# Split gate weights kept in memory for the second half of the tokens, and the MLP's sums and differences of weights and hidden values made by VectorE instead of GpSimd

## The chip, the cores and the metric

One core of a Trainium2 chip runs the kernel. Its time is in device microseconds (us), the median of three runs. Five engines work beside each other: TensorE (PE, matmuls), VectorE (DVE), ScalarE (ACT), GpSimd (POOL), and SyncE (SP), whose queue issues all loads and stores. Each runs its own list of instructions in order and waits on semaphores for the others.

## The reference

A token sequence x (2048 tokens of width 1024) goes through two blocks. What matters here is the first one, between its state-space mixer and its MLP:

```python
def s5_mixer(u, ..., w_glu):
    ...
    y = jax.nn.gelu(y).astype(u.dtype)
    a, g = jnp.split(y @ w_glu, 2, axis=-1)
    return a * jax.nn.sigmoid(g)

def sqrelu_mlp(h, w1, w2):
    a = jax.nn.relu(h @ w1)
    return (a * a) @ w2

x = x + mix
x = x + sqrelu_mlp(rmsnorm(x, norm_ffn[i]), mlp_w1[i], mlp_w2[i])
```

`w_glu` is 1024 x 2048, `w1` 1024 x 4096, `w2` 4096 x 1024, all float32. A second gate (`ple`) and a whole second block of attention, recurrence and convolution follow, which the change doesn't touch.

## The kernel before

**Numbers.** PE gets float16 operands. Each float32 value v is split into hi = float16(v) and lo = float16(v - hi), weights after a factor of 64 (`WS`). A product needs three matmuls: hi hi, hi lo, lo hi (`product`, line 257). ScalarE makes a hi, VectorE the lo (`stt`, line 58, or `sub`, line 50).

**Tokens and tiles.** Tokens come in four blocks n = 0 to 3 of 512 columns (`TB`); rows of x in eight tiles m of 128 (`KT`).

**The mixer's end** (`ssm`, last lines). The generator `mixer` stops twice near its end. `build` (line 146) puts the first products of the gated unit, `gated(0)`, behind the first stop, then lets the mixer finish (`flip`, line 2203, transposes the last eighth of y and splits it), then `gated(1)`.

**The gated unit** (`glu`, line 362). 32 units (m, n): first half n = 0, 1 for all m, second half n = 2, 3. A unit has 48 matmuls into two of the four banks with tag "b" (`gated`, line 351), then a sigmoid by ScalarE (`sg`, line 373), two operations by VectorE that add the gated product to x, and ScalarE's squares for the next norm, which GpSimd sums (`squares`, line 283). A half uses each of the eight gate weight tiles once; class `Weights` loads a tile as two 512 KB pieces (`ws`), and its jobs split it (`prepare`, line 376: four operations on ScalarE, four on VectorE). Since the list of tiles has the eight gate tiles twice (line 168), the second half loads and splits them again.

**What runs beside it.** Three lists of jobs are worked off a few at a time, at places written by hand: `step` (line 249) takes n pending norm jobs and one weight job; `split_aside` (line 487) takes jobs of `presplit` (line 427), which makes the seven combinations of every w2 tile that the MLP needs: subtractions on GpSimd, hi on ScalarE, lo on VectorE, a store to memory `wd_s`. After the first half `norm_pair` (line 558) queues the norm of blocks 0 and 1: first the reciprocal root (`pair_rstd`, line 519, with empty jobs as delay), then 28 parts of a norm, a difference or both, with a cast and a subtraction each.

**The MLP** (`mlp`, line 670) works on two blocks of tokens at a time with seven products in place of eight (the operands of a 2 x 2 block product are combined beforehand by additions and subtractions). Per half of the tokens there are 16 calls of `up` (line 696; I call one a piece: seven products of 12 matmuls into four banks) and eight of `down` (line 753: four times seven products of six matmuls), in the order up, then up, up, down and so on, with one up ahead of the last down. VectorE evicts every product of `down` from its bank (`sums`, line 772). The seven combined weights of a piece are made by `Weights.combine` (line 418): four additions or subtractions (tile `sw`) by `pool` = GpSimd, seven hi by ScalarE, seven lo by VectorE, as ten jobs, called in the `up` before (`steps`) or in the `down` before. The seven combined hidden values need four subtractions more (`less`, line 703), also by `pool`. In both functions the variable `pool` alone decides the engine. `norms` (line 872) takes the norm jobs of the other half of the tokens in every second step of a `down`, so that three downs per half are crowded with them (`norm_away`, line 601, `norm_parked`, line 876).

**Queues.** All loads and stores are issued by SyncE in program order; a store that waits for VectorE holds up what comes behind it.

## Time and profile before

| | before |
|---|---|
| median of three runs | 3205.69 us (3202.18 to 3206.14) |
| the profiled execution | 3202.28 us, span 3200.5 us |
| mean granted clock of TensorE | 0.989 |
| PE busy | 3096.0 us (97%), 16756 matmuls |
| DVE busy | 2177.6 us (68%), 4485 instructions |
| ACT busy | 1308.2 us (41%), 2827 instructions |
| POOL busy | 620.6 us (19%), 482 instructions |

In the span, the mixer's end and the start of the gated unit lie at 233 to 265 us, the gated unit's first half of the tokens ends near 408, its second half near 605; the MLP runs from 608 to 1810, its second half of the tokens from 1215. A busy time is the sum over an engine's instructions; what PE waits for is read from its timeline, where idle time stands in brackets with the instruction that ended it.

### The profile page before, as it was taken

What the parts mean: (1) busy time and instruction counts of PE and PEld (TensorE: products, weight loads), DVE (VectorE), ACT (ScalarE), POOL (GpSimd) and SP (SyncE); (2) the same over time, 40 slices, a digit from 0 to 9 for tenths busy, and PEclk for the clock granted to TensorE, in tenths of its full rate; (3) what the DMA queues carried; (4) which work ended last, traced back from release to release, by engine and by line L of the source; (5) the groups of instructions that cost most, each with busy time, mean ns of one, the idle gap of its engine ahead of it and who ended that gap; (6) DMA issues with size and microseconds to landing.
All of it is one profiled execution on the core that took longest, in us unless ns stands there. A gap on an engine that the chain in (4) does not pass through costs nothing. (4 is left out here: it accounts for less than half of the span.)

```text
span 3200.5 us, 45638 instructions
## 1 busy us (share of the span) xinstructions
PE 3096.0 (97%) x16756; PEld 1593.0 (50%) x16756; DVE 2177.6 (68%) x4485; ACT 1308.2 (41%) x2827; POOL 620.6 (19%) x482
## 2 busy tenths in 40 slices
PE   8889998899999999999999999999999999999999
PEld 6664443344444444444444444654544446666644
DVE  8995668667776667677655655755767866677742
ACT  8983444444444325333333343311212325555610
POOL 0002443332232325322222334200000000000000
PEclk9999999899999999999999999999999999999999
DMA  4136665524342254344322510241121333233242
GB/s 156 52 112 213 212 219 193 175 73 125 112 128 83 76 186 163 89 119 128 98 84 73 185 33 20 75 140 53 63 70 59 108 105 108 82 85 86 81 151 86
DMA packets 294721, 356.94 MB, mean 112 GB/s; under 512 B 44960, under 2 KB 214880, under 8 KB 291296
## 3 DMA queue, kind: packets, MB, share of 16 engines
q1 hardware_dynamic: 289888, 345.63, 34.2%
q10 hardware_dynamic: 4608, 8.39, 0.7%
q8 instruction: 132, 2.16, 0.3%
q14 instruction: 93, 0.76, 0.1%
HBM read 257.98 MB, written 95.94 MB: 111 GB/s over the span
## 5 line engine op out<-in xcount | busy, mean ns | idle before, releaser
L264 PEld LDWEIGHTS <-w 128*128 128x128 f16 x4032 | 396.4, 99 | 502.4 <-issue 35.2
L711 PE MATMUL up<-y,w 128*128 128x512 f16 x2688 | 586.6, 380 | 6.7 <-ACT w L2460 3.4
L768 PE MATMUL dn<-x,w 128*128 128x512 f16 x1764 | 435.0, 381 | 11.3 <-DVE ss L59 5.0
L768 PEld LDWEIGHTS <-w 128*128 128x128 f16 x2688 | 263.9, 98 | 343.5 <-issue 27.9
L711 PEld LDWEIGHTS <-w 128*128 128x128 f16 x2688 | 263.4, 98 | 326.0 <-issue 6.5
L264 PE MATMUL ga<-y,w 128*128 128x512 f16 x1536 | 342.4, 386 | 23.7 <-ACT sg L373 17.9
L59 DVE SCALAR_TENSOR_TENSOR x<-dn,x 128x512 f32<-128x512 f32 x320 | 217.8, 687 | 75.3 <-PE dn L768 70.5
L768 PE MATMUL dn<-y,w 128*128 128x512 f16 x924 | 252.1, 382 | 8.1 <-DMA w<-wd_s 3.2
L41 DVE TENSOR_TENSOR y<-up,y 128x512 f32<-128x512 f32 x128 | 88.4, 690 | 213.2 <-PE up L711 212.0
L59 DVE SCALAR_TENSOR_TENSOR w<-ws,w 128x512 f16<-128x512 f32 x228 | 186.8, 824 | 21.4 <-ACT w L2406 15.3
L1441 PE MATMUL oz<-oz,h 128*128 128x512 f16 x768 | 190.3, 386 | 0.0
L264 PE MATMUL pg<-h,w 128*128 128x512 f16 x768 | 171.4, 379 | 2.5 <-DVE h L41 2.5
L41 POOL TENSOR_TENSOR r<-y,r 128x512 f32<-128x512 f32 x96 | 139.4, 1452 | 159.3 <-DVE x L41 99.0
L1815 PE MATMUL fo<-mx,wo 128*128 128x512 f16 x768 | 167.4, 379 | 0.0
L264 PE MATMUL wide<-w,h 128*128 128x512 f16 x768 | 166.9, 379 | 0.0
L264 PE MATMUL mqk<-h,w 128*128 128x512 f16 x768 | 165.9, 379 | 0.0
L264 PEld LDWEIGHTS <-h 128*128 128x128 f16 x1152 | 112.4, 98 | 99.5 <-DVE gif L59 4.0
L59 DVE SCALAR_TENSOR_TENSOR acc<-u,par,acc 128x512 f32<-128x512 f32 x232 | 159.2, 745 | 0.0
L41 POOL TENSOR_TENSOR sw<-ws 128x512 f32<-128x512 f32 x64 | 89.4, 1397 | 350.8 <-DMA ws<-w 221.6
L41 POOL TENSOR_TENSOR ss<-ss,sq 128x512 f32<-128x512 f32 x70 | 99.1, 1420 | 269.6 <-ACT sq L292 269.6
L2460 ACT ACTIVATE w<-sw 128x512 f16<-128x512 f32 x128 | 79.1, 623 | 126.6 <-POOL sw L41 126.1
L292 ACT ACTIVATE sq<-x 128x512 f32<-128x512 f32 x84 | 51.9, 628 | 176.5 <-DVE x L41 143.3
(402 smaller groups left out, 4753.1 us busy)
## 6 DMA issues: line engine op xcount, KB each, us to landing
w<-wd_s SPq DMA_DIRECT2D x448, 128.0 KB
ws<-w SPq DMA_DIRECT2D x64, 512.0 KB
wd_s<-pw SPq DMA_DIRECT2D x112, 256.0 KB
ws<-wd SPq DMA_DIRECT2D x34, 512.0 KB
ws<-wglu SPq DMA_DIRECT2D x32, 512.0 KB
pw<-w SPq DMA_DIRECT2D x32, 512.0 KB
y<-hop_s SPq DMA_DIRECT2D x20, 512.0 KB
xu<-xu SPq DMA_DIRECT2D x8, 1024.0 KB
```

Source lines behind the costliest of these rows:

```text
L41: f = lambda: (eng or self.nc.vector).tensor_tensor(out=out, in0=in0, in1=in1, op=op)
L59: f = lambda: self.nc.vector.scalar_tensor_tensor(out=out, in0=in0, scalar=s, in1=in1, op0=op0, op1=op1)
L264: self.nc.tensor.matmul(out=ps, lhsT=wk[p], rhs=xk[q], start=(first and i == 0 and j == 0), stop=(last and i == n - 1 and j == 2))
L292: self.nc.scalar.activation(out=sq, in_=x, func=ACT.Square, **kw)
L711: nc.tensor.matmul(out=ps[name], lhsT=ops[o][:, p, 128 * k:128 * k + 128], rhs=self.operand(o, k, q), start=(first and k == 0 and p + q == 0),
L768: nc.tensor.matmul(out=ps[mp, name], lhsT=w[:, 128 * p:128 * p + 128], rhs=x[:, q], start=(opens and c == 0 and p + q == 0), stop=(c == 1 ...
L1441: nc.tensor.matmul(out=d["bank", g], lhsT=x[:, k, s], rhs=y[:, c], start=(k == 0 and j == 0), stop=(k == 7 and j == 2))
L1815: self.nc.tensor.matmul(out=self.begun[m, n], lhsT=w[:, x, c], rhs=y[:, k], start=(k == 0 and j == 0), stop=(k == KT - 1 and j == 2))
L2460: nc.scalar.activation(out=out[q - 2][:, 0], in_=src[q - 2], func=ACT.Copy, scale=scale)
```

## The change

It does four things. (1) The list holds each gate tile once. After its last use in the first half a split tile is stored to a new memory tensor `wg_s` (`keep`), and the second half loads it from there, split (`again`). (2) The second gate tile is split before the mixer's last transposes; a sigmoid on one column stands ahead of the first gate, and the last of the four transposes uses another bank. (3) `pool` in `mlp` and in `Weights.combine` is VectorE; combine's chain is one job shorter, and the first combine is called two units earlier. (4) The pace of the job lists differs: one norm job less per unit from unit 21 on, one presplit job more in units 16 to 21, fewer empty jobs, both reciprocal roots ahead of both spreads.

```diff
-        tiles = [(self.a["wglu"][i], WS) for i in range(KT)] * 2
+        tiles = [(self.a["wglu"][i], WS) for i in range(KT)]
...
         begun = [self.gated(0)]
+        self.weights.prepare(1)
+        self.weights.run()
         next(mixer, None)
         begun.append(self.gated(1))
+        self.nc.scalar.activation(out=self.small[:, 3, 0:1], in_=self.ones[:, 0:1], func=ACT.Sigmoid)
...
-        w = self.weights.get(KT * (n // 2) + m)
+        w = self.weights.get(m) if n < 2 else self.again[m]
...
-            self.step(2)
-            self.split_aside(2)
+            self.step(2 if at < 21 else 1)
+            self.split_aside(3 if 16 <= at < 22 else 2)
...
+        wg_s = nc.dram_tensor("wg_s", [KT, 128, 2, 2048], F16).ap()
+        self.again = {}
+
+        def again(m):
+
+            t = self.wpool.tile([128, 2, 2048], F16, tag=f"w{(KT + m) % 3}", name="w")
+            nc.sync.dma_start(out=t, in_=wg_s[m])
+            self.again[m] = (t[:, 0], t[:, 1])
+
+        def keep(m):
+            for p, t in enumerate(W.get(m)):
+                nc.sync.dma_start(out=wg_s[m, :, p], in_=t)
+
         for half in range(2):
             for m in range(KT):
                 for n in (2 * half, 2 * half + 1):
                     unit(m, n)
                     if n % 2 == 0:
                         i = KT * half + m + 2
-                        if i < 2 * KT:
+                        if i < KT:
                             W.prepare(i)
-                        elif i == 2 * KT + 1:
+                        elif i < 2 * KT:
+                            again(i - KT)
+                        elif i == 2 * KT:
                             self.combined(0)
+                    elif half == 0:
+                        keep(m)
...
-        return [lambda: None] * 3 + [spread, copy]
+        return [lambda: None] * 2 + [spread, copy]
...
-        pool = nc.gpsimd
+        pool = nc.vector
...
-                up(i, (2, 1, 2, 1, 1, 1, 2) if nxt[0] == "up" else (0,) * 7)
+                up(i, (2, 1, 1, 1, 1, 1, 2) if nxt[0] == "up" else (0,) * 7)
...
-        for f in flip(KT - 1, (0, 4, 8, 12), ("a", 3)):
+        for f in flip(KT - 1, (0, 4, 8), ("a", 3)) + flip(KT - 1, (12,), ("c", 1)):
...
-        pool = nc.gpsimd
+        pool = nc.vector
...
+    def run(self):
+        while self.jobs:
+            self.jobs.pop(0)[1]()
```

**Three places of the lists.** ScalarE at the start of the gated unit, before: the last part of the mixer (`GY`, `yt`), the table for the sigmoid, the first gates (`sg`), and between them the second weight tile (`w<-ws`).

```order
L2198 ACTIVATE GY<-y_2730 128x2x16x16
L2216 CAST y_2822<-yt 128x2x64x4 x4
L373 ACT_TABLE_LOAD
L373 ACTIVATE sg<-ga_2779 128x512
L289 ACTIVATE ss<-x_2328 128x512
L2406 ACTIVATE w<-ws 128x512
L373 ACTIVATE sg<-ga_2852 128x512
```

The same place in the change:

```order
L2222 ACTIVATE GY<-y_2730 128x2x16x16
L2430 ACTIVATE w<-ws 128x512 x4
L2240 CAST y_2835<-yt 128x2x64x4 x4
L191 ACT_TABLE_LOAD
L191 ACTIVATE small<-cst 128x1
L377 ACTIVATE sg<-ga_2779 128x512
L292 ACTIVATE ss<-x_2328 128x512
L377 ACTIVATE sg<-ga_2865 128x512
```

All four parts of the second weight tile and the table stand ahead of the first gate now.

ScalarE in the second half of the gated unit, before, from the gate of unit 24 to the gate of unit 25 (casts of line 542 are the norm's, `pw` are presplit's, `w<-ws` gate weights):

```order
L373 ACTIVATE sg<-ga_4839 128x512
L292 ACTIVATE sq<-x_2904 128x512
L542 CAST pw<-nt 128x512
L542 CAST y_2097<-nt 128x512
L477 ACTIVATE pw<-sw 128x4x128 x2
L542 CAST y_2656<-nt 128x512
L2406 ACTIVATE w<-ws 128x512
L477 ACTIVATE pw<-pw 128x4x128
L542 CAST ss<-nt 128x512
L2406 ACTIVATE w<-ws 128x512
L477 ACTIVATE pw<-sw 128x4x128
L373 ACTIVATE sg<-ga_4936 128x512
```

The same two gates in the change:

```order
L377 ACTIVATE sg<-ga_4827 128x512
L295 ACTIVATE sq<-x_2918 128x512
L566 CAST y_2097<-nt 128x512
L499 ACTIVATE pw<-pw 128x4x128
L499 ACTIVATE pw<-sw 128x4x128
L566 CAST y_2656<-nt 128x512
L499 ACTIVATE pw<-sw 128x4x128
L566 CAST ss<-nt 128x512
L499 ACTIVATE pw<-pw 128x4x128
L377 ACTIVATE sg<-ga_4914 128x512
```

The two weight operations are gone, and three norm casts stand where there were four. VectorE's list between the same two gates shrinks from 15 large operations to 12.

VectorE where a `down` (its evictions are `x<-dn`) is followed by a piece (its evictions are `y<-up`), before:

```order
L59 SCALAR_TENSOR_TENSOR x_2910<-dn,x_2910 128x512
L59 SCALAR_TENSOR_TENSOR w<-ws,w 128x512
L41 TENSOR_TENSOR y_2822<-up,y_2822 128x512 x2
L59 SCALAR_TENSOR_TENSOR w<-ws,w 128x512
L59 SCALAR_TENSOR_TENSOR w<-sw,w 128x512 x2
```

The same place in the change:

```order
L59 SCALAR_TENSOR_TENSOR x_2924<-dn,x_2924 128x512
L59 SCALAR_TENSOR_TENSOR w<-ws,w 128x512
L41 TENSOR_TENSOR sw<-ws 128x512
L59 SCALAR_TENSOR_TENSOR w<-ws,w 128x512
L41 TENSOR_TENSOR sw<-sw,ws 128x512
L41 TENSOR_TENSOR y_2835<-up,y_2835 128x512 x2
L59 SCALAR_TENSOR_TENSOR w<-sw,w 128x512 x2
```

Two operations on freshly loaded weights (`sw<-ws`, `sw<-sw,ws`), which were GpSimd's, now stand on VectorE ahead of the piece's first evictions.

## Rows read from the trace of the kernel before

**Rows 1.** Stretches: PE, PEld, DVE, ACT, POOL busy (count), granted clock, DMA share, GB/s.

```profile
265.00:517.00 252.00, 252.00 (x1177) 116.01 (x1176) 177.32 (x230) 108.53 (x194) 105.28 (x71) 0.99 0.64 209
517.00:605.00 88.00, 69.70 (x292) 29.71 (x290) 64.73 (x85) 35.52 (x63) 28.27 (x19) 0.90 0.59 197
605.00:660.00 55.00, 49.28 (x219) 22.00 (x220) 40.69 (x47) 30.02 (x54) 28.26 (x19) 0.94 0.36 107
660.00:1170.00 510.00, 503.41 (x2336) 228.99 (x2334) 350.69 (x532) 199.89 (x343) 145.26 (x107) 1.00 0.37 110
1170.00:1215.00 45.00, 39.08 (x171) 16.81 (x170) 34.70 (x49) 15.61 (x27) 25.82 (x19) 0.96 0.64 211
...
1765.00:1810.00 45.00, 40.11 (x171) 17.13 (x169) 35.77 (x50) 17.66 (x31) 18.99 (x14) 0.92 0.66 217
```

**Rows 2.** Timeline of PE, start of the gated unit: start, us, instruction, [idle before <-releaser].

```profile
260.15 0.60 PE L264 MATMUL ga<-y,w 128*128 128x512 f16 x2 [3.41 <-ACT w L2406]
263.21 37.09 PE L264 MATMUL ga<-y,w 128*128 128x512 f16 x158 [2.46 <-DVE w L59]
```

**Rows 3.** Timeline of PE, end of the gated unit and start of the MLP.

```profile
519.01 10.52 PE L264 MATMUL ga<-y,w 128*128 128x512 f16 x48 [1.21 <-ACT sg L373]
534.42 12.57 PE L264 MATMUL ga<-y,w 128*128 128x512 f16 x48 [4.90 <-ACT sg L373]
548.81 10.52 PE L264 MATMUL ga<-y,w 128*128 128x512 f16 x48 [1.82 <-ACT sg L373]
564.84 12.72 PE L264 MATMUL ga<-y,w 128*128 128x512 f16 x48 [5.51 <-ACT sg L373]
582.01 22.57 PE L264 MATMUL ga<-y,w 128*128 128x512 f16 x96 [4.45 <-ACT sg L373]
607.95 1.03 PE L711 MATMUL up<-y,w 128*128 128x512 f16 x2 [3.38 <-ACT w L2460]
609.39 32.93 PE L711 MATMUL up<-y,w 128*128 128x512 f16 x142 [0.40 <-DVE w L59]
```

**Rows 4.** Stretch of 10 us behind a wait for a sigmoid, columns as in rows 1.

```profile
530.00:540.00 10.00, 5.58 (x17) 2.09 (x17) 8.20 (x11) 4.24 (x8) 3.41 (x2) 0.66 0.35 123
```

**Rows 5.** Timeline of DVE, second half of the gated unit.

```profile
518.99 0.69 DVE L59 SCALAR_TENSOR_TENSOR sg<-ga,sg 128x512 f32<-128x512 f32 x1 [0.49 <-ACT sg L373]
...
530.44 1.75 DVE L41 TENSOR_TENSOR nt<-nt 128x512 f32<-128x512 f32 x1
...
581.99 0.69 DVE L59 SCALAR_TENSOR_TENSOR sg<-ga,sg 128x512 f32<-128x512 f32 x1 [2.36 <-ACT sg L373]
```

**Rows 6.** Groups by line and form: busy us, mean ns of one, idle before.

```profile
L59 DVE SCALAR_TENSOR_TENSOR x<-dn,x 128x512 f32<-128x512 f32 x320 | 217.8, 687 | 75.3 <-PE dn L768 70.5 <-DMA w<-wd_s 1.2 <-DVE x L59 0.5
...
L59 DVE SCALAR_TENSOR_TENSOR w<-ws,w 128x512 f16<-128x512 f32 x228 | 186.8, 824 | 21.4 <-ACT w L2406 15.3 <-ACT w L2460 5.9
...
L41 POOL TENSOR_TENSOR r<-y,r 128x512 f32<-128x512 f32 x96 | 139.4, 1452 | 159.3 <-DVE x L41 99.0 <-DVE y L41 47.3 <-DVE small L41 5.8
```

**Rows 7.** Stretches of a crowded and a plain down call, columns as in rows 1.

```profile
817.00:857.00 40.00, 36.98 (x171) 16.61 (x170) 37.65 (x55) 11.97 (x21) 11.24 (x8) 1.00 0.55 163
...
1043.00:1079.30 36.30, 36.30 (x169) 16.45 (x168) 27.47 (x40) 8.24 (x14) 10.52 (x8) 1.00 0.38 110
```

**Rows 8.** Timelines of DVE and PE at the end of the MLP's first half.

```profile
1179.29 1.08 DVE L41 TENSOR_TENSOR y<-r,y 128x512 f16<-128x512 f32 x1 [2.03 <-ACT y L701]
...
1181.03 1.44 PE L768 MATMUL dn<-x,w 128*128 128x512 f16 x3 [3.12 <-DVE ss L59]
```

**Rows 9.** Timelines of PE, SP and POOL where a piece follows a down call.

```profile
1006.78 3.40 PE L711 MATMUL up<-y,w 128*128 128x512 f16 x15
...
1008.34 0.35 SPq L2373 DMA_DIRECT2D ws<-w  x1
...
1012.20 1.26 POOL L41 TENSOR_TENSOR sw<-ws 128x512 f32<-128x512 f32 x1 [16.82 <-DMA ws<-w]
```

**Rows 10.** Timeline of SP's queue, second half of the gated unit.

```profile
579.66 10.19 SPq L473 DMA_DIRECT2D wd_s<-pw  x3
```

More of the change, by code (lines that the diff above doesn't have):

```diff
@@ L367, in unit @@
         def unit(m, n):
+            at = next(units)
             if m == 0 and n < len(begun):
@@ L377, in unit @@
             self.squares(m, n, m == 0)
-            self.step(2)
-            self.split_aside(2)
+            self.step(2 if at < 21 else 1)
+            self.split_aside(3 if 16 <= at < 22 else 2)
         W.prepare(1)
         self.presplit()
+        units = iter(range(32))
+        wg_s = nc.dram_tensor("wg_s", [KT, 128, 2, 2048], F16).ap()
[7 more added lines that the diff above has]
+                nc.sync.dma_start(out=wg_s[m, :, p], in_=t)
         for half in range(2):
@@ L515, in copy @@
             self.nc.scalar.copy(out=self.rb[n % 2], in_=r["ps"])
-        return [lambda: None] * 3 + [spread, copy]
+        return [lambda: None] * 2 + [spread, copy]
     def pair_rstd(self, na, ss):
-        jobs = [lambda: None] * 4
+        jobs = [lambda: None] * 2
         self.rb = {}
-        for n in (na, na + 1):
-            y = self.r1[:, 4 * n:4 * n + 4]
-            jobs += self.rstd_jobs(ss[n], self.ones[:, 0:1], D, y) + self.spreads(n, y)
+        y = {n: self.r1[:, 4 * n:4 * n + 4] for n in (na, na + 1)}
+        for n in y:
+            jobs += self.rstd_jobs(ss[n], self.ones[:, 0:1], D, y[n])
+        for n in y:
+            jobs += self.spreads(n, y[n])
         return jobs
@@ L850, in mlp @@
                     self.combined(nxt[1])
-                    n = 10
+                    n = 9
                 down(i, n, last, sums_a if i < 8 else sums_b)
@@ L2452, in part @@
         def part(q):
[L2453 to L2454 removed]
+            if q > 1:
+                t, x = out[q - 2], src.pop(q - 2)
                 k.stt(t[:, 1], x, scale, t[:, 0], ALU.mult, ALU.subtract)
[L2456 removed]
+                if q == 8:
                     free(1)
[L2458 to L2460 removed]
+            if 0 < q < 8:
+                out.append(place(q - 1))
+                nc.scalar.activation(out=out[q - 1][:, 0], in_=src[q - 1], func=ACT.Copy, scale=scale)
             if q < 7:
@@ L2464, in part @@
                     free(0)
-        self.jobs += [(i, lambda q=q: part(q)) for q in range(10)]
+        self.jobs += [(i, lambda q=q: part(q)) for q in range(9)]
+    def run(self):
+        while self.jobs:
+            self.jobs.pop(0)[1]()
     def get(self, i):
```

6 lines of the change are left out of this document (removed).

## The prediction

> **What bounds the kernel now.** The first view is the table of stretches [rows 1]. TensorE (PE) is the engine that sets the time: from 265 to 517, through most of the gated unit, it is busy 252.00 of 252.00 us, in the MLP's first half 503.41 of 510. What can be won is the time in which PE stands still or runs slowly, and that sits in few places: 18.3 us idle in the last units of the gated unit (517 to 605, granted clock 0.90 on average), 5.7 us behind it, some 5 us at each of the two ends of an MLP half (1170 and 1765). PE's timeline names the waits. At the start of the gated unit PE waits 3.41 us for ScalarE's and 2.46 us for VectorE's half of the second weight tile [rows 2]. In those last units it waits five times for a sigmoid, 1.21 + 4.90 + 1.82 + 5.51 + 4.45 = 17.89 us, and then 3.38 and 0.40 us for the first weights of the MLP [rows 3]. The granted clock falls to the lower level (1.2 GHz) after such gaps: 0.66 on average between 530 and 540, where PE had just stood still [rows 4]. What this costs is read from PE's rows: 48 matmuls take 10.52 us, but 12.57 and 12.72 behind two gaps [rows 3].
>
> Why the sigmoid is late: VectorE's timeline has the gate products of five following units, the first at 518.99 and the last at 581.99, so 63.0 us for four units, 15.75 us each [rows 5], against 10.5 us of matmuls. VectorE's list has 15 to 18 large operations per unit there, 16.5 on average, thus 0.955 us per operation with all waits. ScalarE's sigmoid stands behind casts that wait for VectorE's results. Part of the 0.955 is GpSimd: beside a GpSimd operation a VectorE operation with two operands in SBUF takes 1.75 us (at 530.44) instead of 0.69 [rows 5].
>
> **The change, part by part** (against the profiled execution: 3202.3 us; the median of the three runs, 3205.7, lies 3.4 above).
>
> *Start of the gated unit.* The second tile is split before the last transposes, in ScalarE time that was idle, and the sigmoid's table is loaded ahead. Gone are 3.41 + 2.46 us, and the slow stretch behind them: 158 matmuls took 37.09 us where 158/48 x 10.52 = 34.6 would do, 2.5 us [rows 2, 3]. Sum 8.4; the unit now waits for banks instead, a few tenths, so I take 8 (bounds 5 to 9).
>
> *Second half of the gated unit.* The split of eight tiles (32 ScalarE, 32 VectorE operations) disappears, and the norm's jobs are spread: three per unit from the end of unit 20 on, instead of four from unit 21 (units counted from 0 to 31). By the new list units 20 to 27 have 11, 13, 12, 13, 12, 13, 12, 12 large VectorE operations, 98 in all: 98 x 0.955 = 93.6 us, against 8 x 10.5 = 84.0 us of matmuls. VectorE thus falls 9.6 us behind, and PE may be one unit ahead (four banks, two per unit), 10.5 us, before it stops. So the waits nearly vanish. What they cost now is 17.89 us, plus the slow stretches 2.05 + 2.20 + 1.5 (22.57 for 96 matmuls, 21.0 when fast) = 23.7 us [rows 3]. At 1.05 us per operation 102.9 - 84.0 - 10.5 = 8.4 us of waits would be left, at 0.9 none: I take 22, which leaves 1.7 (bounds 12 to 23.7).
>
> *Loads and stores.* Instead of 16 loads of 512 KB the second half gets eight of 1 MB: the same bytes. The first half also writes 8.4 MB: 168 us long some 50 GB/s more, on 209 GB/s at a DMA share of 0.64 [rows 1], so about 0.79: hidden. On SyncE's queue the new load of tile m waits for the matmuls of tile m-3, long done when it is its turn, and it has more than two units (21 us) before its first use; the stores wait for nothing new. Cost 0, as long as the queue isn't late by that much.
>
> *First MLP piece.* Its weights are now made from two units earlier on, so 3.38 + 0.40 us and the slow stretch behind (32.93 us for 142 matmuls, 31.1 when fast: 1.8) go [rows 3]: 5.6, I take 5.5 (bounds 2 to 6).
>
> *MLP.* Each of 32 pieces moves eight operations from GpSimd (1.45 us each [rows 6]) to VectorE (0.69): 256 x 0.69 = 177 us more for VectorE in 1200 us. In a plain down call this is hidden: VectorE has 27.47 us of work in 36.30, with seven more operations 32.3 [rows 7]. In the crowded ones (three per half, where a norm runs beside) it is not: 37.65 us in 40, with PE already stopped for 3 us [rows 7], now +4.8 us. Against that, fewer operations are stretched: weight operations take 0.824 on average, those that read a bank 0.687 [rows 6], so some 28 operations with two SBUF operands give back up to 28 x 0.14 = 3.9. That leaves 1 to 2 us per call; PE pays perhaps half of it: six calls, 4.5 us. In the first three pieces VectorE is busy 40.69 of 55 us [rows 1] and gets some 16 operations (11 us): another 1.5. Loss 6 (bounds: gain 4, loss 25).
> At the end of each half the last piece's sums are made in a chain over three engines: VectorE waits 2.03 us for a cast that waits for GpSimd, and PE 3.12 us for the bank behind it [rows 8]. Three GpSimd steps become shorter by some 0.6 us each: 1.8 per half, less what the four new operations take in the first: gain 2 (bounds -2 to 7).
>
> The Trainium skill (SBUF — State Buffer, "Who interferes with whom") calls the port that VectorE and GpSimd share an exclusive lock: the later one stands still for the other's whole instruction. The 1.75 us agree with it at single operations. By that rule the moved operations could free up to 256 x 1.45 = 371 us of VectorE against the 177 us added, and the MLP would gain; this is the second rival.
>
> Sum: 8 + 22 + 0 + 5.5 - 6 + 2 = 31.5 us. 3202.3 - 31.5 = 3170.8; with the 3.4 us to the median **3174 us**.
>
> **Rivals.**
> 1. *The gated unit stays VectorE-bound.* For it: the 0.955 us include presplit's GpSimd subtractions, which stay. At 1.05 us per operation 8.4 us of waits remain and with them two slow stretches (4 us), 12.4 instead of 1.7: 3174 + 11 = 3185.
> 2. *The MLP's own waits go too.* For it: the stretched operations above. Idle there now: 6.6 + 5.9 + 4.9 = 17.4 us [rows 1]. If VectorE gets lighter in effect, these and my loss of 6 go: 3174 - 23 = 3151. Against it: VectorE's evictions read a bank and aren't stretched (0.687 on average [rows 6]).
> 3. *A new wait on VectorE: slower.* GpSimd waited for the weight loads at no cost: after the down call the next piece starts at 1006.78, its second half tile is requested at 1008.34, and GpSimd's addition starts at 1012.20 [rows 9]. Now VectorE makes this addition, and stands still from about 1008.3 to 1012.2, 3.9 us, in 16 pieces, with the evictions of the piece queued behind. The first of these is ready three products (7.8 us) after the start, and PE needs that bank for its sixth product, 13 us after the start; with 3.5 us of work ahead of that, the wait reaches PE if the load lands later than 9.5 us after the start. Measured are 5.4. If it does, each of 16 pieces pays up to 3.9 us: 62 us, 3174 + 62 = 3236. The Trainium skill (Perfetto Trace Analysis, "Optimizing Scalar/DVE Operations") advises to move work to other engines, GpSimd even, where VectorE is saturated, which is the opposite direction; in the crowded calls the trace has VectorE at 37.65 of 40 us [rows 7].
> 4. *The kept tiles come back too late.* In before's second half the queue stands behind stores that wait for VectorE, three of them for 10.19 us [rows 10]. If six of eight loads were late by 4 us, some 24 us would be gone: 3198.
>
> **How the numbers follow.** Forecast 0.55, rivals 0.17, 0.15, 0.07, 0.06. The range reaches from 3159 to 3194: it holds the forecast with its bounds and the first rival, and leaves out most of the second, the third and the fourth. A difference of 0.2% (6.4 us) can be told from none. Faster by more: 0.55 + 0.17 + 0.15 and half of the fourth, 0.90; within: 0.03; slower: 0.07.
>
> **What would show it.** Right: no wait of PE for a weight tile around 260; at most one or two waits for a sigmoid and no fall of the clock between 500 and 600; the first piece without a wait for weights; VectorE's operations in the MLP at 0.69 us, waits of VectorE for weight loads of some 3 us at pieces behind a down call, with PE unaffected; in the crowded down calls PE waits a little longer than before. Wrong: VectorE waits that PE repeats in each piece (third rival), sigmoids that stay late (first), an MLP without any waits (second).

## The result and the profile after

The changed kernel takes 3163.07 us (median of 4 runs, 3160.66 to 3166.15); the kernel before, run beside it, 3204.6 (4 runs). The ratio is 0.9874 (95% interval 0.9862 to 0.9887): 41.5 us faster. Forecast were 3174, in a range from 3159 to 3194. In the profiled executions the span falls from 3200.5 to 3158.9 us, by 41.6.

| | before | after |
|---|---|---|
| mean granted clock of TensorE | 0.989 | 0.995 |
| PE busy | 3096.0 us (97%) | 3081.4 us (98%) |
| DVE busy | 2177.6 us, 4485 instructions | 2248.0 us, 4709 instructions |
| ACT busy | 1308.2 us, 2827 instructions | 1296.6 us, 2796 instructions |
| POOL busy | 620.6 us, 482 instructions | 265.2 us, 226 instructions |

All comparisons below are made by stages. A stage is measured on PE's timeline, from its first matmul to the first of the next stage; the gated unit's units have 48 matmuls each, a piece 84, a down call 168. "Rest of first half" runs from the MLP's second piece to the last down of that half, "second half" from piece 16 to its last down.

| us | to unit 0 | units 0-2 | 3-19 | 20-31 | first piece | rest of first half | its last down | second half | its last down | behind |
|---|---|---|---|---|---|---|---|---|---|---|
| before | 233.3 | 42.6 | 178.6 | 153.4 | 21.3 | 540.7 | 44.6 | 550.5 | 44.7 | 1390.7 |
| after | 233.5 | 32.8 | 178.6 | 135.9 | 18.1 | 536.3 | 43.2 | 547.3 | 42.8 | 1390.4 |
| difference | +0.1 | -9.8 | 0 | -17.4 | -3.1 | -4.5 | -1.5 | -3.2 | -1.9 | -0.3 |

Of the 17.4 us in units 20 to 31, 3.5 belong to the last unit, in which PE no longer waits for the MLP's first weights. So the gated unit gave 23.7 us, the first piece 6.7, the other MLP stages 11.1.

The stretches of the changed kernel that answer to [rows 1, 7] (PE, PEld, DVE, ACT, POOL busy (count), granted clock, DMA share, GB/s): most of the gated unit; its late units; the MLP's first three pieces; a crowded and a plain down call; the two last downs.

```profile
265.00:487.00 222.00, 222.00 (x1046) 102.83 (x1045) 145.19 (x189) 91.25 (x160) 99.28 (x70) 1.00 0.77 261
487.00:581.00 94.00, 85.78 (x387) 38.17 (x386) 83.32 (x100) 39.35 (x70) 33.34 (x21) 0.98 0.55 190
581.00:636.00 55.00, 55.00 (x261) 25.41 (x259) 41.08 (x74) 33.31 (x58) 1.40 (x2) 1.00 0.41 133
711.20:750.40 39.20, 36.57 (x170) 16.43 (x169) 38.76 (x63) 12.03 (x21) 0.00 (x0) 1.00 0.55 153
1008.30:1044.60 36.30, 36.30 (x170) 16.47 (x169) 30.47 (x48) 8.40 (x14) 0.00 (x0) 1.00 0.39 110
1135.20:1178.40 43.20, 39.06 (x170) 16.85 (x169) 37.96 (x55) 15.27 (x26) 14.72 (x10) 0.96 0.64 214
1725.70:1768.50 42.80, 38.87 (x170) 16.85 (x169) 38.10 (x54) 17.73 (x31) 13.71 (x10) 0.96 0.69 227
```

PE is busy without a gap to 487 and again from 581 to 636. What is left lies between 487 and 581 (8.2 us idle), in crowded down calls (2.6 us in the one shown) and at the two ends.

PE's timeline at the start of the gated unit, to be held against [rows 2]: no wait is left, only the last transposes between two runs of products.

```profile
233.47 9.24 PE L267 MATMUL ga<-y,w 128*128 128x512 f16 x42
242.54 1.91 PE L2236 MATMUL yt<-cst,GY 128*128 128x128 f32 x16
244.29 167.22 PE L267 MATMUL ga<-y,w 128*128 128x512 f16 x774
```

PE's timeline at the gated unit's end and the MLP's start, to be held against [rows 3]: the five waits for a sigmoid are shorter, not gone (1.16 + 2.42 + 1.47 + 2.38 + 0.79 = 8.22 us instead of 17.89), one slow unit is left (12.21 us for 48 matmuls), and the MLP's first piece starts without a wait.

```profile
498.94 10.52 PE L267 MATMUL ga<-y,w 128*128 128x512 f16 x48 [1.16 <-ACT sg L377]
511.88 10.52 PE L267 MATMUL ga<-y,w 128*128 128x512 f16 x48 [2.42 <-ACT sg L377]
523.87 10.52 PE L267 MATMUL ga<-y,w 128*128 128x512 f16 x48 [1.47 <-ACT sg L377]
536.77 12.21 PE L267 MATMUL ga<-y,w 128*128 128x512 f16 x48 [2.38 <-ACT sg L377]
549.77 31.24 PE L267 MATMUL ga<-y,w 128*128 128x512 f16 x144 [0.79 <-ACT sg L377]
580.84 26.06 PE L735 MATMUL up<-y,w 128*128 128x512 f16 x120
```

Two readings of the new profile raise the questions. First, why VectorE is still late in the gated unit. It already comes late into it: the gate product of unit 20 stands at 461.32, 5.9 us behind the end of that unit's matmuls. ScalarE's and GpSimd's timelines there:

```profile
452.25 0.63 ACT L499 ACTIVATE pw<-pw 128x512 f16<-128x512 f32 x1 [4.47 <-DMA wd_s<-pw]
...
460.18 0.63 ACT L499 ACTIVATE pw<-sw 128x512 f16<-128x512 f32 x1 [3.79 <-POOL sw L41]
460.71 0.58 ACT L377 ACTIVATE sg<-ga 128x512 f32<-128x512 f32 x1
```

```profile
458.88 1.27 POOL L41 TENSOR_TENSOR sw<-pw 128x512 f32<-128x512 f32 x1 [9.01 <-DMA pw<-w]
```

`presplit` (three jobs per unit now) waits here for its own stores and loads, and the sigmoid stands behind its casts. That is not new in kind: between 265 and 475 us ScalarE's `pw` operations waited 59.0 us for these stores before, and 61.4 us now.

Second, why the MLP got faster by 11.1 us behind its first piece, where the forecast was 4 us slower.

### The profile page after: what moved, and what is told of

It is laid out like the page before. It is cut to its first block, busy times and chain, and to the rows that moved or that the text cites. A ratio compares the mean times of both kernels' runs of the same rounds, so it can differ in the third digit from the quotient of the medians.

```text
span 3158.9 us, 45408 instructions
## 1 busy us (share of the span) xinstructions
PE 3081.4 (98%) x16756; PEld 1589.5 (50%) x16756; DVE 2248.0 (71%) x4709; ACT 1296.6 (41%) x2796; POOL 265.2 (8%) x226
## 5 line engine op out<-in xcount | busy, mean ns | idle before, releaser
L792 PEld LDWEIGHTS <-w 128*128 128x128 f16 x2688 | 263.7, 98 | 335.7 <-issue 21.3
L267 PE MATMUL ga<-y,w 128*128 128x512 f16 x1536 | 335.0, 380 | 8.2 <-ACT sg L377 8.2
L41 DVE TENSOR_TENSOR y<-up,y 128x512 f32<-128x512 f32 x128 | 88.4, 691 | 117.9 <-PE up L735 116.5
L267 PEld LDWEIGHTS <-h 128*128 128x128 f16 x1152 | 112.3, 98 | 99.5 <-DVE gif L59 4.0
L59 DVE SCALAR_TENSOR_TENSOR w<-ws,w 128x512 f16<-128x512 f32 x196 | 147.5, 758 | 17.2 <-ACT w L2430 15.9
L1839 PEld LDWEIGHTS <-wo 128*128 128x128 f16 x768 | 75.0, 98 | 88.6
L1465 PEld LDWEIGHTS <-h 128*128 128x128 f16 x768 | 71.4, 99 | 68.4 <-issue 3.8
```

The costliest lines, as they stand in the source:

```text
L41: f = lambda: (eng or self.nc.vector).tensor_tensor(out=out, in0=in0, in1=in1, op=op)
L59: f = lambda: self.nc.vector.scalar_tensor_tensor(out=out, in0=in0, scalar=s, in1=in1, op0=op0, op1=op1)
L267: self.nc.tensor.matmul(out=ps, lhsT=wk[p], rhs=xk[q], start=(first and i == 0 and j == 0), stop=(last and i == n - 1 and j == 2))
L792: nc.tensor.matmul(out=ps[mp, name], lhsT=w[:, 128 * p:128 * p + 128], rhs=x[:, q], start=(opens and c == 0 and p + q == 0), stop=(c == 1 ...
L1465: nc.tensor.matmul(out=d["bank", g], lhsT=x[:, k, s], rhs=y[:, c], start=(k == 0 and j == 0), stop=(k == 7 and j == 2))
L1839: self.nc.tensor.matmul(out=self.begun[m, n], lhsT=w[:, x, c], rhs=y[:, k], start=(k == 0 and j == 0), stop=(k == KT - 1 and j == 2))
```

## The experiments

The runs differ behind the MLP too, where nothing was changed (1390.4 to 1397.9 us in these profiles), and the same kernel's last down of a half took 43.2 us in one execution and 41.5 in another. How far one profile can be trusted is seen where several run the same code. Six have the MLP of the changed kernel (after, e4 to e7, e9): it took 1186.0 to 1188.5 us, its second half without the last down 547.3 in all six. Five have its gated unit (after, e1, e3, e9, e10): units 20 to 31 took 134.6 to 136.8 us. So verdicts rest on the stages, read with this play, and the medians stand beside them.

| us | units 0-2 | 3-19 | 20-31 | first piece | rest of first half | its last down | second half | its last down | median (ratio to before, interval) |
|---|---|---|---|---|---|---|---|---|---|
| before | 42.6 | 178.6 | 153.4 | 21.3 | 540.7 | 44.6 | 550.5 | 44.7 | |
| after | 32.8 | 178.6 | 135.9 | 18.1 | 536.3 | 43.2 | 547.3 | 42.8 | 3163.1 (0.9874, 0.9862 to 0.9887) |
| e1 | 32.8 | 178.6 | 134.6 | 19.3 | 537.7 | 44.6 | 547.3 | 45.0 | 3170.5 (0.9893, 0.9877 to 0.9910) |
| e2 | 41.3 | 178.6 | 152.9 | 22.1 | 537.2 | 42.8 | 549.4 | 43.1 | 3193.5 (0.9971, 0.9959 to 0.9983) |
| e3 | 32.8 | 178.6 | 134.8 | 21.1 | 545.2 | 44.3 | 551.7 | 41.3 | 3180.4 (0.9930, 0.9912 to 0.9947) |
| e4 | 32.8 | 185.9 | 142.5 | 18.1 | 535.9 | 41.8 | 547.3 | 43.1 | 3175.6 (0.9916, 0.9902 to 0.9931) |
| e5 | 32.9 | 178.6 | 128.9 | 18.1 | 538.2 | 41.5 | 547.3 | 43.1 | 3156.2 (0.9861, 0.9846 to 0.9876) |
| e6 | 32.8 | 178.6 | 140.5 | 18.1 | 536.9 | 43.2 | 547.3 | 42.8 | 3169.3 (0.9900, 0.9883 to 0.9916) |
| e7 | 32.8 | 191.7 | 134.0 | 18.1 | 537.1 | 43.2 | 547.3 | 42.8 | 3170.3 (0.9902, 0.9887 to 0.9917) |
| e8 | 32.8 | 178.8 | 139.6 | 25.2 | 535.8 | 41.5 | 548.2 | 41.3 | 3173.0 (0.9908, 0.9893 to 0.9923) |
| e9 | 32.8 | 178.6 | 136.2 | 18.1 | 536.0 | 41.5 | 547.3 | 43.1 | 3162.6 (0.9869, 0.9854 to 0.9883) |
| e10 | 32.8 | 178.6 | 136.8 | 18.1 | 536.1 | 45.1 | 548.6 | 45.1 | 3168.5 (0.9885, 0.9868 to 0.9901) |
| e11 | 32.8 | 178.6 | 129.0 | 18.1 | 531.1 | 43.0 | 547.3 | 43.0 | 3152.1 (0.9836, 0.9822 to 0.9851) |
| e12 | 32.8 | 178.6 | 126.8 | 18.1 | 530.8 | 41.6 | 547.3 | 42.6 | 3145.9 (0.9821, 0.9806 to 0.9835) |

### e1 and e2: the engine of the MLP's sums alone

e1 is the changed kernel with `pool` as it was in both places; e2 the kernel before with only that moved.

```diff
 # e1, on the changed kernel (mlp and Weights.combine)
-        pool = nc.vector
+        pool = nc.gpsimd
 # e2, on the kernel before (mlp and Weights.combine)
-        pool = nc.gpsimd
+        pool = nc.vector
```

> The changed kernel with the sums and differences of the MLP back on GpSimd, nothing else undone. Theory A (the MLP gained because GpSimd's operations no longer stretch VectorE's and no longer stand in its chains): the MLP, 1187.6 us in the changed kernel's profile, goes back to 1196 to 1201, its ends from 43.2 and 42.8 to about 44.7 us each, and the median from 3163 to 3171 to 3176. Theory B (the MLP gained because the norm's jobs lie earlier and both reciprocal roots come first; the engine costs what the prediction said, some 4 us net): the MLP comes to 1183 to 1188, the median to 3159 to 3163.

> The kernel before with only the engine of these sums changed to VectorE. Theory A: 8 to 12 us faster than before (3193 to 3197), all of it in the MLP; the gated unit stays at 374.6 us from its first product to the MLP's. Theory B: no faster, 3204 to 3209.

Neither theory holds alone, though e2's median lies in A's range. In e1 the MLP takes 1193.8 us, between the two forecasts: 6.2 of its 14.2 us go back, and the other 8.0 stay. In e2 7.2 us come in the MLP (1201.8 to 1194.6) and 1.8 in the gated unit, and the median falls by 9.3. So the engine is worth 6 to 7 us in the MLP, where the play is 2.5. About half of that, 3.6 us in e1 and 3.4 in e2, lies in the last downs. VectorE's timeline there, in e1: the three waits of [rows 8]'s place are those of the kernel before (2.02, 1.81 and 2.03 us).

```profile
1139.22 0.69 DVE L41 TENSOR_TENSOR y<-y,y 128x512 f16<-128x512 f32 x1 [2.02 <-ACT y L718]
...
1142.91 0.69 DVE L41 TENSOR_TENSOR y<-r,y 128x512 f16<-128x512 f32 x1 [1.80 <-ACT y L725]
1145.63 1.09 DVE L41 TENSOR_TENSOR y<-r,y 128x512 f16<-128x512 f32 x1 [2.02 <-ACT y L725]
```

In the changed kernel two shorter ones are left:

```profile
1138.13 0.69 DVE L41 TENSOR_TENSOR y<-y,y 128x512 f16<-128x512 f32 x1 [1.42 <-ACT y L718]
1143.54 0.69 DVE L41 TENSOR_TENSOR y<-r,y 128x512 f16<-128x512 f32 x1 [0.68 <-ACT y L725]
```

The page of the profile gives the moved operations' price. VectorE's line in e1 and in the changed kernel:

```profile
PE 3086.5 (97%) x16756; PEld 1591.2 (50%) x16756; DVE 2166.2 (68%) x4453; ACT 1291.8 (41%) x2796; POOL 624.8 (20%) x482
```

```profile
PE 3081.4 (98%) x16756; PEld 1589.5 (50%) x16756; DVE 2248.0 (71%) x4709; ACT 1296.6 (41%) x2796; POOL 265.2 (8%) x226
```

256 more instructions cost VectorE 81.8 us of busy time, 0.32 us each and not 0.69: an operation takes 0.605 us from its start to the next one's, which makes 155 us, and most of the other 73 us is stretching that went with GpSimd's operations. (Summed over VectorE's operations of 0.9 to 1.9 us on the two timelines, the time above 0.7 us falls from 143.2 to 80.5 us.)

### e3: GpSimd's operations beside the changed kernel

Each moved operation gets two idle GpSimd additions beside it, on a tile that nobody else uses.

```diff
+        self.idle = const.tile([128, 256], F16, name="idle")
...
-            less = lambda out, x, y: (lambda: self.sub(out, x, y, pool))
+            less = lambda out, x, y: (lambda: (self.sub(out, x, y, pool), beside()))
+            beside = lambda: [self.add(self.idle, self.idle, hid[0][:, 0, c:c + 256], nc.gpsimd) for c in (0, 256)]
...
+            if q in (2, 3, 5, 6):
+                h = out[q - 2][:, 0]
+                [k.add(k.idle, k.idle, h[:, c:c + 256], nc.gpsimd) for c in (0, 256)]
```

> The changed kernel with idle GpSimd additions beside it in the MLP: two of 256 columns behind each of the eight moved operations of a piece, on operands that are there anyway, and nobody waits for them. If the stretching of VectorE by GpSimd is what was won (A1): GpSimd busy some 300 us more, VectorE operations of 1.3 to 1.8 us again, and the MLP 8 us or more longer, the median 3171 or more. If it was the length of GpSimd's steps in the chains in which VectorE stands (A2): at most 2 us longer, 3161 to 3165.

A1: the MLP takes 1203.6 us, 16 more than in the changed kernel, with nobody waiting for the additions. They came out dearer than what they stand for. GpSimd's groups of e3 (the last column: idle before, and what ended it) sum to 445.6 us, where the operations that were moved take 256 x 1.45 = 371 [rows 6]:

```profile
L41 POOL TENSOR_TENSOR idle<-idle,w 128x256 f16<-128x256 f16 x256 | 213.1, 832 | 517.7 <-ACT w L2487 505.8
L41 POOL TENSOR_TENSOR idle<-idle,x 128x256 f16<-128x256 f16 x168 | 152.7, 909 | 91.1 <-ACT x L720 78.7
L41 POOL TENSOR_TENSOR idle<-idle,y 128x256 f16<-128x256 f16 x88 | 79.8, 907 | 63.4 <-ACT y L720 57.0
```

Of the 16 us 11.5 lie in three pieces at the start of the halves (21.1, 23.3 and 23.1 us in place of 18.1, 18.9 and 18.9), where PE waits 2.1 to 2.5 us for VectorE's evictions, and 4.3 in the three crowded downs. VectorE's and PE's timelines in one of those: two operations take 1.15 us in place of 0.69, and PE stops.

```profile
733.80 1.16 DVE L41 TENSOR_TENSOR nt<-x,nt 128x512 f16<-128x512 f32 x1
734.88 1.15 DVE L41 TENSOR_TENSOR x<-x,x 128x512 f32<-128x512 f32 x1
```

```profile
733.33 0.81 PE L795 MATMUL dn<-x,w 128*128 128x512 f16 x3 [1.66 <-DVE ss L59]
736.68 0.81 PE L795 MATMUL dn<-x,w 128*128 128x512 f16 x3 [1.89 <-DVE x L59]
```

The last downs together did not get longer by it (85.6 us; 86.0 in the changed kernel, 84.6 in e9), and VectorE's two waits in the first one are those of the changed kernel, 1.42 and 0.68 us. So stretching costs time where VectorE is crowded, and the ends gain by something else, which the waits of e1 point to: the length of the steps.

### e10: which of the eight operations

```diff
 # mlp only
-        pool = nc.vector
+        pool = nc.gpsimd
```

> The changed kernel with the four subtractions of the hidden values alone back on GpSimd; the weights' four stay on VectorE. With all eight back (e1) the MLP took 1193.8 us instead of 1187.6. If it is the hidden values' chain (subtraction, cast, low part, all at the end of a piece and the start of the down) that pays, nearly all of the 6.2 us comes back: 1192 to 1194 and the two ends above 44 us. If each GpSimd operation costs the same: about half, 1190 to 1191. If it is the weights': 1188.

The hidden values: the MLP takes 1193.0 us and both last downs 45.1. VectorE's waits in the first of them are again 2.02, 1.81 and 2.02 us. These subtractions stand in a chain (subtraction, ScalarE's cast, VectorE's low part), and a step of 0.69 us in place of 1.26 to 1.65 shortens it; the weights' operations are made well ahead, and their engine is worth little.

### e8: the order of the reciprocal roots

```diff
-        jobs = [lambda: None] * 2
+        jobs = [lambda: None] * 4
         self.rb = {}
-        y = {n: self.r1[:, 4 * n:4 * n + 4] for n in (na, na + 1)}
-        for n in y:
-            jobs += self.rstd_jobs(ss[n], self.ones[:, 0:1], D, y[n])
-        for n in y:
-            jobs += self.spreads(n, y[n])
+        for n in (na, na + 1):
+            y = self.r1[:, 4 * n:4 * n + 4]
+            jobs += self.rstd_jobs(ss[n], self.ones[:, 0:1], D, y) + self.spreads(n, y)
...
-        return [lambda: None] * 2 + [spread, copy]
+        return [lambda: None] * 3 + [spread, copy]
```

> The changed kernel with the order of the reciprocal roots as before (root and spread of one block, then of the other, with the longer delays), everything else as changed. With the engine alone undone (e1) the second half's calls of the MLP kept their gain (547.3 against 550.5 us) and the three pieces behind the first kept half of theirs. If the order of the roots gives that part: the calls from the second half's first piece to its last down come to 549 to 551 us, the first half's to 462 or more, the median 3166 to 3169. If it gives nothing: 547.3, and the median within 2 us of the changed kernel's 3163.

The second half came out between the two forecasts (548.2 us), the rest of the first half shows no loss at all (535.8), and the median lies far above both, for a reason that neither had. In the gated unit the norm's last cast now comes at 588.8 us instead of 574.9, the loads that bring its operands back from memory are issued at 593.6 instead of 577.9, and the first piece waits for them (25.2 us); units 20 to 31 take 139.6. The longest of these waits on PE's timeline:

```profile
598.77 1.47 PE L733 MATMUL up<-y,w 128*128 128x512 f16 x6 [2.95 <-DMA y<-hop_s]
```

For the second half it still answers the question, together with e1 and e2: 550.5 us with the old order and GpSimd, 549.4 and 548.2 with the old order and VectorE (e2, e8), 547.3 with the new order and either engine (e1, after). The parts don't add up: everything but the engine (e1) takes all of these 3.2 us away, the engine alone (e2) 1.1, and the old order beside VectorE (e8) costs 0.9. A count on VectorE's timeline shows what the order, with its fewer empty jobs, does there. The norm has 16 parts. With the old order 4, 5 and 5 of them fall into the three crowded downs, with the new one 4, 4 and 3, and five fall into pieces. Over the base of 36.26 us PE loses 2.5 us in these downs before, 0.5 in e2 and in e8, nothing in e1 and after. (e1 also keeps combine's shorter chain, so the order isn't alone in it.)

How the remaining 4.8 us that e1 kept (1.9 in the first piece, 3.1 in the rest of the first half, less 0.2 at the ends) divide between the order and the earlier start was not tried.

### e6: the gate weights split again

```diff
-        tiles = [(self.a["wglu"][i], WS) for i in range(KT)]
+        tiles = [(self.a["wglu"][i], WS) for i in range(KT)] * 2
...
-        w = self.weights.get(m) if n < 2 else self.again[m]
+        w = self.weights.get(KT * (n // 2) + m)
...
-                        if i < KT:
+                        if i < 2 * KT:
                             W.prepare(i)
-                        elif i < 2 * KT:
-                            again(i - KT)
...
-                    elif half == 0:
-                        keep(m)
```

> The changed kernel with the first part undone: the gate weights are loaded and split again in the second half, nothing is kept in memory; pace, engines and the early tile stay. By the prediction's sum (8 tiles with 4 operations on VectorE each at 0.955 us, over 11 units) units 20 to 31 need about 20 to 25 us more than the changed kernel's 135.9, that is 155 to 160, and the median is 3183 to 3188. If the slower pace of the norm is what mattered and the kept weights little: 138 to 142 us, the median 3165 to 3169.

The rival: units 20 to 31 take 140.5 us, 4.6 more than in the changed kernel (3.7 to 5.9, taken against all five profiles of its gated unit). The kept weights, the change's headline, give about 5 us of 41.5. Of the other 12.9 us (153.4 to 140.5) 3.5 belong to the last unit and the earlier first combine; 9.3 are left for the rest of the change, above all the pace and the order of the lists, which were not taken apart here.

### e4 and e5: presplit's sums on VectorE

```diff
 # e4, in presplit's source()
-            P = nc.gpsimd
+            P = nc.vector
 # e5: as e4, but
-                self.add(x, at(1, 0), at(1, 1), P)
+                self.add(x, at(1, 0), at(1, 1), nc.gpsimd)
```

> The changed kernel with the four sums and differences of presplit (the w2 tiles, made beside the gated unit) on VectorE as well. In units 24 to 27 of the changed kernel 13 operations of GpSimd stand beside 13 of VectorE that are stretched by 1.0 us each, 9 of them presplit's. If the stretching is what keeps the sigmoids late: each operation costs VectorE 0.61 us and takes 1.0 us away, 3.5 us over these four units; the five waits for a sigmoid (8.2 us) shrink to 5 or less, and the median falls to 3156 to 3160. If the number of VectorE's operations is what counts: 9 more operations of 0.61 us are 5.5 us more waits over these units, the median 3168 to 3173.

> As e4, but the one sum of presplit that reads a weight half just loaded stays on GpSimd; the three other operations are on VectorE. If e4 lost its time because VectorE, in place of GpSimd, stood waiting for the loads of w2 (thirteen waits of 1 to 6 us in its trace), while the stretching was worth what was said: no wait of VectorE for these loads, the first half of the gated unit back at 10.36 us per unit, and units 20 to 31 at 133 us or less (135.9 in the changed kernel); the median 3156 to 3162. If it lost because VectorE has more operations to do: units 20 to 31 stay at 140 or more, the median 3168 to 3174.

e4 became slower than the changed kernel, above the forecast of either theory, and half of the loss lies in a stage that had no waits (units 3 to 19: 185.9 us, 7.3 more). VectorE's and PE's timelines there:

```profile
385.59 0.69 DVE L41 TENSOR_TENSOR sw<-pw 128x512 f32<-128x512 f32 x1 [5.38 <-DMA pw<-w]
```

```profile
397.49 20.88 PE L267 MATMUL ga<-y,w 128*128 128x512 f16 x96 [2.48 <-ACT sg L377]
```

In its groups VectorE stands 54.9 us before these operations, where GpSimd had stood at no cost. e5 leaves the one operation that meets a fresh load on GpSimd, and both of its numbers come out: 178.6 us for units 3 to 19, and 128.9 for units 20 to 31, 7.0 less than the changed kernel. PE's timeline of e5, all waits of the gated unit:

```profile
531.10 10.52 PE L267 MATMUL ga<-y,w 128*128 128x512 f16 x48 [1.33 <-ACT sg L377]
543.52 31.24 PE L267 MATMUL ga<-y,w 128*128 128x512 f16 x144 [1.90 <-ACT sg L377]
```

### e7: presplit's faster pace earlier

```diff
-            self.split_aside(3 if 16 <= at < 22 else 2)
+            self.split_aside(3 if 4 <= at < 10 else 2)
```

> The changed kernel with the six units in which presplit takes one job more moved from units 16 to 21 to units 4 to 9. In the changed kernel VectorE comes into unit 20 with its gate product 5.9 us late, behind ScalarE, which waits 4.47 us for a store and 3.79 us for GpSimd, which waits 9.01 us for a load of w2. If these waits of the faster pace are what the prediction missed: the lag at unit 20 falls to 3 us or less, the waits for a sigmoid from 8.2 us to 4 or less, the median to 3156 to 3160. If the lag comes from the reciprocal roots that stand there, or if the earlier units can't take the faster pace: no gain, or a wait in the first half, 3162 to 3170.

No gain. VectorE's lag at unit 20 falls from 5.9 to 3.9 us and units 20 to 31 from 135.9 to 134.0, but the waits for a sigmoid stay (1.85 + 1.47 + 2.38 + 2.49 us), and the earlier units lose 13 us: ScalarE waits there for presplit's stores, up to 5.2 us at a time. The five profiles of the changed gated unit have lags of 4.7 to 6.2 us and take 134.6 to 136.8 us, a microsecond more for about a microsecond of lag, and e7 lies on the same line. So the faster pace cost about 1 to 2 us of the miss, not most of it.

### e9, e11 and e12: the changed kernel again, and a faster one

e9 is the changed kernel. e11 adds to e5 an empty job between any two parts of the norm in the first half's down calls; e12 adds to that the sums of squares on VectorE, half a unit later.

```diff
 # e11, norm_away
-            jobs += wait + [lambda k=k, q=q: part(k, q) for q in range(5)]
-            jobs += wait + [lambda k=k, q=q: part(k, q) for q in range(5, 8)]
+            for q in range(8):
+                jobs += wait if q in (0, 5) else wait[:1]
+                jobs.append(lambda k=k, q=q: part(k, q))
 # e12 also, in squares and glu
...
-            self.add(ss, ss, sq, self.nc.gpsimd)
+            add = lambda: self.add(ss, ss, sq, self.nc.vector if late is not None else self.nc.gpsimd)
+            add() if late is None else late.append(add)
...
-                ps = self.gated(n, m, range(KT), between=lambda i: (self.step(), self.split_aside()))
+                ps = self.gated(n, m, range(KT), between=lambda i: (self.step(), self.split_aside(), done()))
...
+        def done():
+            while late:
+                late.pop()()
...
```

> The changed kernel itself, as the measure for the three beside it on the same chip: 3160 to 3167.

> As e5, and in the MLP's first half the norm's parts, which come in runs of five and three, with an empty job between any two. In e5 and in the changed kernel VectorE falls behind in the three crowded down calls (in the changed kernel 39.2, 37.3 and 39.4 us instead of 36.26). If it is the bunching of the norm's parts: these calls come to 36.3 to 37 us, the MLP to 1182 to 1184, the median 4 to 6 us below e5's 3156: 3150 to 3153. If the norm's work is only pushed into calls that have no room for it either: the MLP stays at 1187 to 1190, the median 3155 to 3159.

> As e11, and the sums of the squares beside the gated unit on VectorE too, half a unit later. By the price that the runs so far give (0.61 us for an operation of VectorE, 1.0 us for one of GpSimd beside it) 0.4 us less per unit: units 20 to 31 from 128.9 us in e5 to 126 to 127.5, the median 1.5 to 3 us below e11. If VectorE then stands waiting for the squares: 129 to 132, the median above e11.

Both came out as the first theory of each said. In e11 the three crowded calls take 36.9, 36.3 and 36.3 us, the next one, crowded now too, 37.3, and the MLP 1182.6. The empty jobs spread the same work over more calls: VectorE has 60, 58, 59, 59 and 53 large operations in five calls in a row, where the changed kernel has 63, 59, 63, 48 and 48. In e12 units 20 to 31 take 126.8 us, 2.1 to 2.2 less than in e5 and e11, which is no more than the play; its median falls by 6.3 us where 1.5 to 3 were expected, but of that 1.8 lie at the last downs and 1.9 behind the MLP, where e12 changes nothing. PE's timeline has two short waits left:

```profile
529.36 10.52 PE L267 MATMUL ga<-y,w 128*128 128x512 f16 x48 [0.47 <-ACT sg L378]
540.70 31.24 PE L267 MATMUL ga<-y,w 128*128 128x512 f16 x144 [0.82 <-ACT sg L378]
```

e12 takes 3145.9 us beside 3162.6 for the changed kernel on the same chip, and its slowest execution (3151.5) lies below the other's fastest (3161.2). It beats both kernels. Its lines for the engines:

```profile
PE 3076.0 (98%) x16756; PEld 1587.5 (51%) x16756; DVE 2241.1 (71%) x4785; ACT 1299.2 (41%) x2796; POOL 152.6 (5%) x150
```

VectorE has 76 instructions more than in the changed kernel and is busy 6.9 us less.

## Why the prediction was right, and where not

The direction and the range were right. The sum of its gains (31.5 us, measured 41.6) was off in two large steps of opposite sign: the gated unit's second half gave 8 us less, the MLP nearly 14 us more. That the time came into the range is in part luck: with the 22 us of the gated unit and all else as measured it would have been 3155, below the range.

**Start of the gated unit** (forecast 8, measured 9.8): as forecast in mechanism, a little above the upper bound of 9; the few tenths of waits for banks didn't come. e2, which runs the code of before there, took 41.3 us instead of 42.6, so 1.3 us are play.

**Second half of the gated unit** (forecast 22, measured 13.9 in units 20 to 30): mis-sized by 8 us, and the failed step is "98 x 0.955 = 93.6 us", one average price for every operation of VectorE. From the gate product of unit 20 to that of unit 27, worked out from the timelines of VectorE and GpSimd (large operations, of 128x512; stretched means over 0.9 us, idle are gaps over 0.15 us; PE alone needs 72.5 us there):

| units 20 to 27 | VectorE's operations | GpSimd's | stretched | time above 0.7 us in these | VectorE idle | took |
|---|---|---|---|---|---|---|
| before | 101 | 23 | 20 | 16.5 us | 14.6 us | 97.0 us |
| after | 86 | 24 | 22 | 22.7 us | 9.5 us | 88.4 us |
| e6 (split again) | 99 | 24 | 22 | 20.7 us | 8.5 us | 92.9 us |
| e5 | 99 | 11 | 9 | 8.5 us | 10.3 us | 83.1 us |
| e12 | 106 | 4 | 3 | 2.8 us | 11.5 us | 82.3 us |

e5 and e6 have the same 99 operations, and e5 is 9.8 us faster. Before, 97.0 us for 101 operations were indeed 0.96 each, but a third of that (31.1 us) was stretching and idle time, which belong to GpSimd's operations and to waits for ScalarE, and did not leave with the operations that the change removed (32.2 us after). The count of operations was right: 98 in eight units were forecast, and 86 in seven came. But thirteen fewer (e6 to after) were worth 4.5 us, 0.35 each and not 0.955. The stretched operation and GpSimd's operation beside it, in the changed kernel:

```profile
508.40 1.75 DVE L41 TENSOR_TENSOR nt<-ss,nt 128x512 f32<-128x512 f32 x1
```

```profile
507.85 1.76 POOL L41 TENSOR_TENSOR sw<-pw 128x512 f32<-128x512 f32 x1 [2.55 <-DVE pw L59]
```

The Trainium skill (SBUF — State Buffer, "Who interferes with whom") has VectorE's second port and GpSimd exclude each other. The trace agrees: nearly every GpSimd operation has its stretched one (22 of 24), though VectorE loses 22.7 us to 38.0 us of GpSimd's, not all of it. The first rival (1.05 us per operation, 12.4 us left, 3185) named the right place and nearly the size: 1.03 us per operation (88.4 / 86) and 9.9 us left (8.22 us of waits and 1.7 of a slow unit). Only its time didn't come, because other terms gave more.

**Loads and stores** (forecast 0): wrong by 1 to 2 us, which are part of the same 8. The kept tiles came in time, so the fourth rival didn't come, and the estimated DMA share of 0.79 came to 0.77. But presplit at its faster pace stood longer behind its own loads and stores, and VectorE entered unit 20 late by 5.9 us (2.7 before), which the sum had at 0. With the faster pace elsewhere (e7) the lag is 3.9 us.

**First MLP piece** (forecast 5.5, measured 6.7): as forecast in mechanism, a little above the upper bound of 6.

**MLP** (forecast a loss of 6; measured a gain of 7.7, behind the first piece and without the last downs): the sign was wrong, and the gain lies outside the bounds (gain 4, loss 25). The load was estimated well: a crowded call came to 38.76 us of VectorE in 39.2, from 37.65 [rows 7], 1.1 us more where "1 to 2 us per call" stood. What failed is the step from there, "PE pays perhaps half of it; six calls, 4.5 us", which rested on no row, and the 1.5 us more for the first three pieces. The gain of 7.7 us lies in both places. Part of it is in the second piece of each half, where PE waited for evictions before and no longer does: 2.7 and 0.7 us over the bare matmuls. The rest is in the crowded downs: 1.8 us in the first half and 2.5 in the second.

In the second half the three crowded downs hold 56, 56 and 55 large operations of VectorE, 34 us at 0.605 us each, under the 36.26 us that PE needs, and PE doesn't wait. Before, VectorE was busy no longer in such a call, and PE did wait (0.64 us for a late result of VectorE and 0.70 for a load in the one shown). The first line is a crowded down of before, the second one of after:

```profile
1418.15:1456.10 37.95, 36.61 (x170) 16.36 (x169) 33.74 (x49) 10.30 (x18) 10.78 (x8) 1.00 0.56 160
1308.70:1345.00 36.30, 36.30 (x170) 16.46 (x169) 34.67 (x56) 11.24 (x20) 0.00 (x0) 1.00 0.58 162
```

So the busy time of a call says little as long as it stays below PE's. What counts there is how many of the norm's parts a call gets (5 and 4 in these two), and GpSimd's operations beside them, as the runs under e8 show. In the first half the load itself is too large in two calls of three: 63, 59 and 63 operations are 38.1, 35.7 and 38.1 us at 0.605, and the calls take 39.2, 37.3 and 39.4. e11, which spreads them over five calls, takes 5 us away there (531.1 against 536.0 in e9; e5, on which it builds, took 538.2) with the same work. The diff's part (4) was priced only in the gated unit.

One wait in these calls was overlooked throughout, and it is not VectorE's: PE also stops for `w2` tiles that `down` loads. In the changed kernel SyncE's queue issues ten of these loads in a row from 875.49 on, right behind a store and three loads of the norm. In the first half's crowded downs that is 3.23 us of 6.5 before, and 0.87 + 1.08 us of 6.1 in the changed kernel. PE's timeline, before and after:

```profile
925.00 1.46 PE L768 MATMUL dn<-y,w 128*128 128x512 f16 x3 [3.23 <-DMA w<-wd_s]
```

```profile
880.54 0.82 PE L792 MATMUL dn<-y,w 128*128 128x512 f16 x3 [1.08 <-DMA w<-wd_s]
```

**The ends** (forecast 2, measured 3.4): right in mechanism (e10), with 1.7 us of play between executions of one kernel.

**Second rival** (an MLP without any waits, 3151): partly true. Its mechanism, VectorE set free by GpSimd's absence, is shown by e3 in the other direction, but by itself the engine gave 6 to 7 us (e1, e2), half of them at the ends and by shorter steps, and not 23.

**Third rival** (slower by a new wait on VectorE): its mechanism came to the letter and its price wasn't paid. VectorE's group of these additions, and its timeline at one piece:

```profile
L41 DVE TENSOR_TENSOR sw<-ws 128x512 f32<-128x512 f32 x64 | 45.6, 713 | 62.8 <-DMA ws<-w 60.5 <-DMA xk_s<-x 2.3
```

```profile
977.77 0.69 DVE L41 TENSOR_TENSOR sw<-ws 128x512 f32<-128x512 f32 x1 [4.23 <-DMA ws<-w]
...
980.02 1.42 DVE L41 TENSOR_TENSOR y<-up,y 128x512 f32<-128x512 f32 x2 [0.35 <-PE up L735]
```

VectorE stands still for 62.8 us in all, the 16 x 3.9 us of the prediction. The piece starts at 972.05, the load has landed 5.7 us later, under the 9.5 us from which PE would pay, and the evictions wait for PE and not PE for them. e4 shows the other side: the same kind of wait, 54.9 us of it beside the gated unit, costs PE 7 us in the first 20 units. The advice of the Trainium skill that the prediction quotes with this rival (Perfetto Trace Analysis, "Optimizing Scalar/DVE Operations") comes there with the warning that moving work between VectorE and GpSimd might not help; here the move to VectorE paid (e1, e2).

Of what would show the forecast right, the start, the first piece and the waits of some 3 us came. "At most one or two waits for a sigmoid and no fall of the clock" did not: five are left, with one slow unit, 12.21 us. That PE waits a little longer in the crowded downs came in the first half alone, and for VectorE alone (4.2 us instead of 3.3); with the loads it waits 6.1 us there instead of 6.5, and in the second half not at all.

## What to carry to other kernels

Price a removed operation by what leaves with it: its own start-to-start time (0.605 us here), and separately the stretching (about 1 us per GpSimd operation beside a crowded VectorE, 22.7 us for 24) and the waits, which stay if their cause stays. Before moving an operation from an idle engine to a busy one, ask what it waits for: an operation that meets a fresh load costs nothing on an idle GpSimd and stops everything behind it on VectorE. Where the next result is due later than the load (the MLP here) that is harmless; where it isn't (e4), move the others and leave that one. In a diff with several parts the pace and the order of the job lists can be worth more than the headline: here the kept weights gave about 5 us of 41.5.

## What was not expected of the hardware

The stretching differs with the form of GpSimd's operations. Beside additions of 128x512 in float32 (1.3 to 1.8 us) VectorE's stretched operations took 1.35 to 1.78 us in units 20 to 27, most of them 1.75; beside additions of 128x256 in float16, whose records show 0.83 to 0.91 us on average, most took 1.15 (e3). Size and type were changed together, so which of them counts is open. And VectorE's records overlap: an operation of 0.69 us is followed by the next one 0.605 us after its start, so that the sum of durations (56 x 0.69 = 38.6 us) can exceed a stretch of 36.3 in which the engine is busy 34.67 and keeps up.
